# All late output projections moved ahead of the first up-projection, and the token operands of the second pair of chunks made early and kept in DRAM

## The chip, the cores and the metric

The kernel runs on one core of a Trainium2 chip. The metric is the device time of one execution in microseconds (us), as the median of several runs. TensorE is called PE below, VectorE DVE, ScalarE ACT, GpSimd POOL, and SyncE, whose queue issues every DMA of this kernel, SP.

## The reference, cut to what matters

One encoder layer on x of 2048 tokens x 1024 features, float32 throughout:

```python
mix = token_mixer(x, w_in, b_forget, rel_bias, w_out)   # two kinds of attention, 16 heads; y = heads; y @ w_out
x = layer_norm(alpha * x + mix, ln1_g, ln1_b)           # "norm 1"
u = x @ w_up                                            # (1024, 5632)
u = sum(shift(u, j) * conv_w[j] for j in range(3)) + conv_b   # causal, along the tokens
value, gate = split(u, 2)
ffn = (value * gelu(gate)) @ w_down                     # (2816, 1024)
x = layer_norm(alpha * x + ffn, ln2_g, ln2_b)
```

## The kernel before, in words

**Products.** Every float32 operand of a large product is split in two parts of a reduced float32 format (`split`: ACT copies the high part, L177; DVE or POOL subtracts it from the source for the low part, L180), and `mm3` (L184 to L186) makes three matmuls of 128x128 by 128x512 for each product of tiles. A tile is 128 x 512 float32, 256 KB. Which of DVE and POOL makes a low part or a sum is decided while the program is written out, by `choice`, which keeps an estimated load for both.

**Tokens.** The 2048 tokens are four chunks of 512 (0 to 3). Attention comes first, woven with the input projection and then with the output projections of chunks 0 and 1 (`dense_work`, L1221). What remains of this dense work when the attention has been written out, some 41 yields of eight to an output step, is run by the loop `while dense.step()` near the end of the file.

**Output projection.** `out_steps(c)` gives eight steps (2 halves of the columns by 4 blocks of 128 tokens), each of 24 matmuls. Its first step's `load` fetches eight tile pairs of `w_out` (from the DRAM copy `wo_d`, L769) and eight tiles of the attention's output (`y_d`, L777); its `prepare` splits the eight y tiles; its `multiply` does the matmuls and adds the residual. The last step calls `done`, which queues `out_norm(c)` as chores: four for the norm itself (L832, L815, L817, L818, store to `x1_d`), and eight with four PE transposes each (L841), whose results are stored to `x1t_d` in DRAM, tokens along the free axis.

**Up-projection.** `ffn_up2(ca)` multiplies two chunks at once in seven products instead of eight (a Strassen form). It needs seven sets of four token operands: `tokens_step(n)`, for n = 1, 5, 6, 3, 7, 2, 4, loads four tiles of `x1t_d` (L916) for four of the n, makes differences for four of the n (`subtract`, L904), and splits four tiles. These 28 pairs of parts stay in fast memory through the whole up-projection: 22 blocks of seven product steps, each step 12 matmuls. A block loads four tiles of `w_up` (L1012), makes sums of them (L987) and splits, convolves (L855 to L857) and stores h to `h_d`. `ffn_down2(ca)` follows with 77 steps of 12 matmuls, with weights from `wd_d` (L1134) and h from `h_d` (L1131); its norm is `finish` (L1100 to L1115), run as chores.

**Order.** `Pipeline` runs a list of steps. Before step i it calls `load` of steps up to i+5 (beyond i+2 only if enough slots are free) and `prepare` up to i+2; after step i it pops one chore (more in the first seven steps, `PACE`). The list before is: out steps of chunk 2, up-projection of chunks 0 and 1, out steps of chunk 3, down-projection of chunks 0 and 1, up-projection of chunks 2 and 3, down-projection of chunks 2 and 3. The token steps stand in it at positions `FPOS` around the first step of the first up-projection and at `XPOS` (-6, -4, -2, 0, 1, 2, 3) around that of the second. `OLEAD` is the length of the leading part.

**Slots.** All these tiles live in 85 numbered slots (`Slots`): 54 that exist from the start, and 31 on the right side that are added when the attention's buffers go, at the end of the attention, with a key 40 counts later. `get` takes the free slot with the oldest key (`mem.next = 0`). A new user of a slot waits for the last reader of the one before.

**An early start that is written in.** While the remaining dense work runs, `if n == FIRST` (60) would load and split for the first step of the pipeline, from the far end of the list of free slots.

Of the kernel before, what the change touches and what calls it, by code (L numbers as in the profile page):

```python
# [19 lines left out]
P = 128  # L20
# [5 lines left out]
CH = 512  # L26
# [70 lines left out]
OLEAD = 8  # L97
RIGHT_T, FIRST = 40, 60
# [8 lines left out]
def hymba_layer(  # L107
# [61 lines left out]
    wd_d = tl(dram, [NF // 2, 8, 2, P, CH], F32, "wd_d")  # L169

# [589 lines left out]
    def out_steps(c, mem, zp, banks, state, done):  # L760
# [9 lines left out]

        def product_step(j, t):
            def load():
                if (j, t) == (0, 0):
                    load_tiles(0, range(KT))
                    for k in range(KT):
                        ys.append(mem.get())
                        nc.sync.dma_start(ys[k], y_d[k, :, cs])  # L777
                if (j, t) == (0, TQ - 1):
                    load_tiles(1, range(WNEXT))

            def prepare():
                if (j, t) == (0, 0):
                    state["z"] = [{} for _ in range(TQ)]
                    state["stt"] = tl(zp, [P, TQ, 2, 6], F32, "bn", 2)
                    for k, raw in enumerate(ys):
                        ys[k] = mem.get(F32R), mem.get(F32R)
                        split(*ys[k], raw, nc.scalar, nc.vector)
                        mem.put(raw)
# [31 lines left out]
    def out_norm(c, mem, zp, banks, sink, gains, state):  # L820
# [8 lines left out]
        for t in range(TQ):  # L829
            for j in range(2):  # L830
# [4 lines left out]
                nc.sync.dma_start(x1_d[r0 : r0 + P, CH * j : CH * j + CH], zj)  # L835
            yield YT
# [59 lines left out]
    def ffn_up2(ca, fs, mem, banks, before, wide):  # L896

        HK = KT // 2  # L900
        xs = {}
# [4 lines left out]
        b, t2 = {}, {}  # L906

        def tokens_step(n):


            def load():
                for i, q in {1: ((0, 0),), 5: ((0, 1),), 6: ((1, 1),), 2: ((1, 0),)}.get(n, ()):
                    for k in range(HK):
                        before(ca + q, HK * i + k)
                        b[i, q, k] = mem.get()
                        nc.sync.dma_start(f32(b[i, q, k]), x1t_d[ca + q, HK * i + k])  # L916

            def source(k):

                b00, b01, b10, b11 = (b.get((i, q, k)) for i in range(2) for q in range(2))  # L920
                if n == 1:
                    return b00, ()
                if n == 5:
                    t2[k] = b00
                    subtract(b00, b01, b00)
                    return b00, ()
                if n == 6:
                    subtract(t2[k], b11, t2[k])
                    return t2[k], ()
                if n == 3:  # L930
                    return b11, ()
                if n == 7:
                    subtract(b01, b11, b01)
                    return b01, (b01, b11)
                if n == 2:
                    return b10, ()
                subtract(t2[k], b10, t2[k])
                return t2[k], (t2[k], b10)

            def prepare():  # L940
                for k in range(HK):
                    src, last = source(k)
                    xs[n, k] = mem.get(F32R), mem.get(F32R)
                    split(*xs[n, k], f32(src), nc.scalar, choice.engine())
                    mem.put(*last)
# [229 lines left out]
    with ExitStack() as st:  # L1175
# [16 lines left out]
        written = set()  # L1192
# [18 lines left out]
        def normed(c, state):  # L1211
            def done():
                later(out_norm(c, mem, zp, banks, to_dram(c), gains, state), KT + TQ + 1)
                if c == NCH - 1:
                    chores.append(load_norms)
            return done
# [50 lines left out]
        for c in range(2, NCH):  # L1267
            state = {}
            outs.append(out_steps(c, mem, zp, banks, state, normed(c, state)))
        outs = outs[0] + outs[1]  # L1270
# [85 lines left out]
```

## Time and profile before

| | us |
|---|---|
| median of three runs | 2845.57 (2844.66 to 2853.41) |
| profiled execution | 2845.75 |
| its span, first to last instruction | 2843.8 |
| PE busy in the span | 2740.9 (96%) |
| DVE busy | 1933.6 (68%) |
| ACT busy | 1175.7 (41%) |
| POOL busy | 897.4 (32%) |

The 1.95 us between the profiled execution's time and its span lie outside the first and last instruction. PE is busy almost everywhere, but a matmul's recorded time overlaps that of the next one, so what a stretch loses is better read from how many matmuls it holds than from its busy share. Times in the rows are counted from the start of the span. The weight load of PE (PEld) is a row of its own in the views. The granted clock (PEclk) is 1.00 where PE has its full 2.4 GHz.

### The profile page before, as it was taken

To read this page: it belongs to the slowest core of one execution; us is meant where nothing else is said; L and a number is where in the kernel's file an instruction comes from. 1 tells how busy PE (TensorE), PEld (TensorE's weight loads), DVE (VectorE), ACT (ScalarE), POOL (GpSimd) and SP (SyncE) were. 2 spreads that over 40 slices of the span, in tenths; PEclk is the share of its full clock that TensorE was granted. 3 is DMA by queue.
4 is the path that set the end of the run, shared out by engine and by line. 5 is a ranking of instruction groups with operands and counts; after the bars stand their busy time and mean duration, and the time that the engine had idled before them with its cause. 6 is when DMAs were issued, how large, how long until landed. Compare 5 with 4: busy or idle time off the path is not lost.

```text
span 2843.8 us, 38496 instructions
## 1 busy us (share of the span) xinstructions
PE 2740.9 (96%) x12632; PEld 2046.2 (72%) x12632; DVE 1933.6 (68%) x3391; ACT 1175.7 (41%) x2036; POOL 897.4 (32%) x940
## 2 busy tenths in 40 slices
PE   8899999999999999999879999999998999999998
PEld 7675757675666766765657888888876778888886
DVE  4456576767676755567587777765569877777548
ACT  4434344444444443424245544542223545544222
POOL 2224242426557554334152112111026311110012
PEclk9999999999999999999999999999999999999999
DMA  7665667765456445767842222279873322226964
GB/s 236 197 208 179 204 189 222 217 190 184 149 167 195 151 130 152 214 187 232 296 156 78 81 87 78 78 247 327 296 229 114 104 78 84 83 78 206 316 221 163
DMA packets 308487, 498.01 MB, mean 175 GB/s; under 512 B 68896, under 2 KB 84384, under 8 KB 308288
## 3 DMA queue, kind: packets, MB, share of 16 engines
q1 hardware_dynamic: 308288, 495.56, 55.3%
q8 instruction: 100, 1.64, 0.2%
q14 instruction: 99, 0.81, 0.1%
HBM read 347.97 MB, written 147.46 MB: 174 GB/s over the span
## 4 chain that ended last, share of the span: by engine, by line
PE 64%; DVE 6%; issue 3%; DMA 3%; POOL 2%; ACT 1%; SPq 0%; POOLq 0%; DVEq 0%; ACTq 0%
PE acc L184 17%; PE acc L186 17%; PE acc L185 17%; PE y L705 5%; PE sc L581 3%; PE st L618 3%; PE st L619 2%; DVE slot L180 2%; DMA qb<-qh_d 1%; DVE slot L1109 1%; PE sc L657 1%; DMA slot<-y_d 1%; DVE slot L815 1%; ACT slot L177 0%; PE acc L841 0%
## 5 line engine op out<-in xcount | busy, mean ns | idle before, releaser
L184 PE MATMUL acc<-slot,slot 128*128 128x512 f32 (+2 forms) x3128 | 1189.6, 380 | 46.3 <-ACT slot L177 30.2
L186 PE MATMUL acc<-slot,slot 128*128 128x512 f32 (+2 forms) x3128 | 1184.5, 379 | 12.2 <-DVE slot L180 10.6
L185 PE MATMUL acc<-slot,slot 128*128 128x512 f32 (+2 forms) x3128 | 1182.3, 378 | 0.0
L184 PEld LDWEIGHTS acc<-slot,slot 128*128 128x128 f32 x3128 | 594.2, 190 | 171.6 <-ACT slot L177 35.8
L177 ACT ACTIVATE slot<-slot 128x512 fp32r<-128x512 f32 (+1 forms) x688 | 410.3, 622 | 730.0 <-DVE slot L1079 143.2
L186 PEld LDWEIGHTS acc<-slot,slot 128*128 128x128 f32 x3128 | 592.8, 190 | 138.5 <-DVE slot L180 20.0
L185 PEld LDWEIGHTS acc<-slot,slot 128*128 128x128 f32 x3128 | 594.0, 190 | 113.4 <-issue 3.2
L180 DVE TENSOR_TENSOR slot<-slot,slot 128x512 fp32r<-128x512 f32 (+1 forms) x548 | 448.2, 828 | 255.4 <-ACT slot L177 227.1
L639 POOL TENSOR_TENSOR sums<-sums,pt 128x512 f32<-128x512 f32 (+3 forms) x416 | 421.2, 1012 | 237.8 <-ACT pt L630 182.7
L630 ACT ACTIVATE pt<-st 128x512 f32<-128x512 f32 (+3 forms) x544 | 262.2, 492 | 329.6 <-PE st L619 119.2
L180 POOL TENSOR_TENSOR slot<-slot,slot 128x512 fp32r<-128x512 f32 (+1 forms) x144 | 197.6, 1374 | 304.1 <-ACT slot L177 249.0
L705 PE MATMUL y<-pt,vv 128*64 128x512 f32 (+3 forms) x1088 | 280.3, 505 | 0.2 <-DVE yt L647 0.2
L618 PE MATMUL st<-qa,ka 128*128 128x512 f32 (+2 forms) x544 | 208.5, 386 | 8.3 <-ACT pt L630 8.3
L581 PE MATMUL sc<-kb,qb 66*128 66x512 f32 (+2 forms) x544 | 186.8, 373 | 11.8 <-DMA qb<-qh_d 5.2
L619 PE MATMUL st<-qb,kb 97*128 97x512 f32 (+2 forms) x544 | 189.9, 357 | 3.7 <-ACT qb L599 3.3
L584 DVE TENSOR_REDUCE mx<-sc 128x1 f32<-128x512 f32 x192 | 127.8, 685 | 74.5 <-PE sc L581 73.3
L618 PEld LDWEIGHTS st<-qa,ka 128*128 128x128 f32 x544 | 102.5, 189 | 96.8 <-issue 43.7
L705 PEld LDWEIGHTS y<-pt,vv 128*64 128x64 f32 x1088 | 81.6, 136 | 120.4 <-issue 105.1
L856 DVE SCALAR_TENSOR_TENSOR v<-u,cw,v 128x1024 f32<-128x1024 f32 x88 | 113.5, 1290 | 76.4 <-ACT v L855 76.3
L581 PEld LDWEIGHTS sc<-kb,qb 66*128 66x128 f32 x544 | 98.9, 190 | 83.5 <-DVE mx L589 19.8
L639 POOL TENSOR_TENSOR sums<-pt 128x384 f32<-128x384 f32 (+1 forms) x64 | 78.7, 1229 | 251.4 <-PE sc L657 194.8
L589 DVE CUSTOM_DVE_ANT_0 junk<-sc,bq 128x512 bf16<-128x512 f32 (+2 forms) x224 | 108.3, 483 | 47.8 <-PE sc L581 39.0
(113 smaller groups left out, 2263.9 us busy)
## 6 DMA issues: line engine op xcount, KB each, us to landing
slot<-wd_d SPq DMA_DIRECT2D x308, 256.0 KB
slot<-in_w_up_dram SPq DMA_DIRECT2D x176, 256.0 KB
wd_d<-w_hl SPq DMA_DIRECT2D x77, 512.0 KB
slot<-wo_d SPq DMA_DIRECT2D x128, 256.0 KB
h_d<-v SPq DMA_DIRECT2D x44, 512.0 KB
slot<-h_d SPq DMA_DIRECT2D x88, 256.0 KB
slot<-in_w_qk_dram SPq DMA_DIRECT2D x66, 256.0 KB
kb<-kh_d SPq DMA_DIRECT2D x88, 128.0 KB
```

What stands on the lines that cost most here:

```text
L177: nc.scalar.activation(hi, src, AF.Copy)
L180: lo_eng.tensor_tensor(lo, src, f32(hi), op=ALU.subtract)
L184: nc.tensor.matmul(acc, wh, mh, start=first, stop=False, **more)
L185: nc.tensor.matmul(acc, wh, ml, start=False, stop=False, **more)
L186: nc.tensor.matmul(acc, wl, mh, start=False, stop=last, **more)
L581: nc.tensor.matmul(sc[:, m0:m1], qb[:KR, tq], kb[:KR, m0:m1], start=True, stop=True)
L584: nc.vector.tensor_reduce(m, sc[:, k0:k1], axis=AX.X, op=ALU.max)
L618: nc.tensor.matmul(st[:, w2], ka[:, js], qa[:, w2], start=True, stop=False)
L619: nc.tensor.matmul(st[:, w2], kb[:KM, js], qb[:KM, w2], start=False, stop=True)
L630: nc.scalar.activation(pt[:, w], st[:, w], AF.Exp)
L639: nc.gpsimd.tensor_tensor(acc[:, w], (acc if first is None else first)[:, w], pt[:, w], op=ALU.add)
L705: nc.tensor.matmul(y[half, w], v, pt[:, w], start=first and n < 2, stop=last and n >= len(tiles) - 2)
```

## The change

All sixteen output steps of chunks 2 and 3 now stand ahead of the first up-projection, in one list. `out_norm` yields twice more between its norm and its transposes (`NORM_LAG`), and that of chunk 3 is popped at every second step. After it, chores at every third step (`XEVERY`) run a new generator, `store_tokens(2)`: it loads the 16 tiles of chunks 2 and 3 from `x1t_d`, makes the seven sets of operands, splits them, and stores the 56 parts to a new DRAM tensor `xq_d`. The token steps of the second up-projection only load these 56 parts. Making the operands has become a function, `token_operands`, which both users share. `FIRST` is 12 instead of 60, and what happens there is only the loading and splitting of chunk 2's y tiles (`load_y`, `split_y`), from the near end of the list of free slots; the `wo_d` tiles are loaded by the pipeline's own first step.

The part left out of the diff is the old body of `source`, which stands again, with n as an argument, in `token_operands`.

```diff
--- before.py
+++ after.py
@@ -94,8 +94,9 @@
 EV1, EV0 = 2, 3
 PACE = 5, 5, 3, 2, 2, 2, 2
 FPOS = -1, 0, 1, 2, 3, 4, 5
-OLEAD = 8
-RIGHT_T, FIRST = 40, 60
+XEVERY = 3
+RIGHT_T, FIRST = 40, 12
+NORM_LAG = 2
 XPOS = -6, -4, -2, 0, 1, 2, 3


@@ -167,6 +168,8 @@

     wo_d = tl(dram, [KT, 2, 2, P, CH], F32, "wo_d")
     wd_d = tl(dram, [NF // 2, 8, 2, P, CH], F32, "wd_d")
+
+    xq_d = tl(dram, [8, KT // 2, 2, P, CH], F32, "xq_d")

     halo = tl(consts, [P, 2, NF, 2], F32, "halo")
     cw = tl(consts, [P, 2, NF, 4], F32, "cw")
@@ -768,24 +771,33 @@
                 for n in range(2):
                     nc.sync.dma_start(f32(ws[j, k][n]), wo_d[k, j, n])

+        def load_y():
+            for k in range(KT):
+                ys.append(mem.get())
+                nc.sync.dma_start(ys[k], y_d[k, :, cs])
+
+        def split_y():
+            state["z"] = [{} for _ in range(TQ)]
+            state["stt"] = tl(zp, [P, TQ, 2, 6], F32, "bn", 2)
+            for k, raw in enumerate(ys):
+                ys[k] = mem.get(F32R), mem.get(F32R)
+                split(*ys[k], raw, nc.scalar, nc.vector)
+                mem.put(raw)
+
+        state["early"] = load_y, split_y
+
         def product_step(j, t):
             def load():
                 if (j, t) == (0, 0):
                     load_tiles(0, range(KT))
-                    for k in range(KT):
-                        ys.append(mem.get())
-                        nc.sync.dma_start(ys[k], y_d[k, :, cs])
+                    if not ys:
+                        load_y()
                 if (j, t) == (0, TQ - 1):
                     load_tiles(1, range(WNEXT))

             def prepare():
-                if (j, t) == (0, 0):
-                    state["z"] = [{} for _ in range(TQ)]
-                    state["stt"] = tl(zp, [P, TQ, 2, 6], F32, "bn", 2)
-                    for k, raw in enumerate(ys):
-                        ys[k] = mem.get(F32R), mem.get(F32R)
-                        split(*ys[k], raw, nc.scalar, nc.vector)
-                        mem.put(raw)
+                if (j, t) == (0, 0) and "z" not in state:
+                    split_y()

             def multiply():
                 acc = banks.get()
@@ -834,6 +846,8 @@
                 r0 = c * CH + t * P
                 nc.sync.dma_start(x1_d[r0 : r0 + P, CH * j : CH * j + CH], zj)
             yield YT
+        for _ in range(NORM_LAG):
+            yield YT
         for k in range(KT):
             tps = banks.get()
             for t in range(TQ):
@@ -893,56 +907,101 @@
     def nothing():
         pass

-    def ffn_up2(ca, fs, mem, banks, before, wide):
-
-
-
-        HK = KT // 2
-        xs = {}
+    HK = KT // 2
+
+    def token_operands(ca, ks, mem, before, dst):
+
+
+        b, t2 = {}, {}

         def subtract(o, x, y):
             choice.engine().tensor_tensor(f32(o), f32(x), f32(y), op=ALU.subtract)

-        b, t2 = {}, {}
+        def load(i, q):
+            for k in ks:
+                before(ca + q, HK * i + k)
+                b[i, q, k] = mem.get()
+                nc.sync.dma_start(f32(b[i, q, k]), x1t_d[ca + q, HK * i + k])
+
+        def source(n, k):
+
+            b00, b01, b10, b11 = (b.get((i, q, k)) for i in range(2) for q in range(2))
+            if n == 1:
+                return b00, ()
+            if n == 5:
+                t2[k] = b00
+                subtract(b00, b01, b00)
+                return b00, ()
+            if n == 6:
+                subtract(t2[k], b11, t2[k])
+                return t2[k], ()
+            if n == 3:
+                return b11, ()
+            if n == 7:
+                subtract(b01, b11, b01)
+                return b01, (b01, b11)
+            if n == 2:
+                return b10, ()
+            subtract(t2[k], b10, t2[k])
+            return t2[k], (t2[k], b10)
+
+        def load_for(n):
+            for i, q in {1: ((0, 0),), 5: ((0, 1),), 6: ((1, 1),), 2: ((1, 0),)}.get(n, ()):
+                load(i, q)
+
+        def prepare(n):
+            for k in ks:
+                src, last = source(n, k)
+                parts = mem.get(F32R), mem.get(F32R)
+                split(*parts, f32(src), nc.scalar, choice.engine())
+                mem.put(*last)
+                dst(n, k, parts)
+
+        return load_for, prepare
+
+    def store_tokens(ca, mem, before, stored):
+
+
+        def dst(n, k, parts):
+            for l in range(2):
+                nc.sync.dma_start(xq_d[n, k, l], f32(parts[l]))
+            mem.put(*parts, delay=DLY_E)
+            stored.add((n, k))
+
+        for k in range(HK):
+            load, prepare = token_operands(ca, [k], mem, before, dst)
+            for n in UP_ORDER:
+                load(n)
+            for n in UP_ORDER:
+                yield
+                prepare(n)
+
+    def ffn_up2(ca, fs, mem, banks, before, wide, stored):
+
+
+
+        xs = {}
+
+        def keep(n, k, parts):
+            xs[n, k] = parts
+
+        load_tokens, prepare_tokens = token_operands(ca, range(HK), mem, before, keep)

         def tokens_step(n):


             def load():
-                for i, q in {1: ((0, 0),), 5: ((0, 1),), 6: ((1, 1),), 2: ((1, 0),)}.get(n, ()):
-                    for k in range(HK):
-                        before(ca + q, HK * i + k)
-                        b[i, q, k] = mem.get()
-                        nc.sync.dma_start(f32(b[i, q, k]), x1t_d[ca + q, HK * i + k])
-
...
             def prepare():
-                for k in range(HK):
-                    src, last = source(k)
-                    xs[n, k] = mem.get(F32R), mem.get(F32R)
-                    split(*xs[n, k], f32(src), nc.scalar, choice.engine())
-                    mem.put(*last)
+                if not stored:
+                    prepare_tokens(n)

             return Step(load, prepare, nothing, 12 if n in (1, 5, 6, 2) else 8, 0)

@@ -1189,7 +1248,7 @@
                 written.add((c, k))
             return sink

-        written = set()
+        written, stored = set(), set()

         def before(c, k):

@@ -1210,9 +1269,10 @@

         def normed(c, state):
             def done():
-                later(out_norm(c, mem, zp, banks, to_dram(c), gains, state), KT + TQ + 1)
+                later(out_norm(c, mem, zp, banks, to_dram(c), gains, state), KT + TQ + NORM_LAG + 1, 2 if c == NCH - 1 else 1)
                 if c == NCH - 1:
                     chores.append(load_norms)
+                    later(store_tokens(2, mem, before, stored), HK * (len(UP_ORDER) + 1), XEVERY)
             return done

         def dense_work():
@@ -1265,26 +1325,24 @@

         outs = []
         for c in range(2, NCH):
-            state = {}
-            outs.append(out_steps(c, mem, zp, banks, state, normed(c, state)))
-        outs = outs[0] + outs[1]
-        first, up01 = ffn_up2(0, range(NF), mem, banks, before, wide)
-        second, up23 = ffn_up2(2, range(NF), mem, banks, before, wide)
-        lead = place(outs[:OLEAD] + up01, first, [OLEAD + i for i in FPOS])
+            part = {}
+            outs += out_steps(c, mem, zp, banks, part, normed(c, part))
+            if c == 2:
+                early = part["early"]
+        first, up01 = ffn_up2(0, range(NF), mem, banks, before, wide, False)
+        second, up23 = ffn_up2(2, range(NF), mem, banks, before, wide, True)
+        lead = place(outs + up01, first, [len(outs) + i for i in FPOS])
         down01 = ffn_down2(0, mem, zp, banks, gains, later, False)
         down23 = ffn_down2(2, mem, zp, banks, gains, later, True)
         rest = place(down01 + up23, second, [len(down01) + i for i in XPOS])
-        work = Pipeline(mem, lead + outs[OLEAD:] + rest + down23, chores)
+        work = Pipeline(mem, lead + rest + down23, chores)
         mem.add(st.enter_context(tc.tile_pool(name="r_s", bufs=1, **side)), SLOTS_B, RIGHT_T)
         n = 0
         while dense.step():
             n += 1
             if n == FIRST:
-                mem.next = -1
-                work.ahead(-AHEAD_L)
-                work.steps[0].prepare()
-                work.prepared = 1
-                mem.next = 0
+                for fn in early:
+                    fn()
         banks.add(st.enter_context(tc.tile_pool(name="r_ps", bufs=8 - DACC, space=PSUM, **side)), 8 - DACC)
         work.run()
```

## Rows read from the trace of the kernel before

**Rows 1.** The page, part 1: busy us, share and instructions of two engines.
```profile
PE 2740.9 (96%) x12632; PEld 2046.2 (72%) x12632; DVE 1933.6 (68%) x3391; ACT 1175.7 (41%) x2036; POOL 897.4 (32%) x940
```

**Rows 2.** Windows of 50 us: length, PE, PEld, DVE, ACT, POOL busy (count), PEclk, DMA.
```profile
1700.00:1750.00 50.00, 50.00 (x217) 40.51 (x216) 38.29 (x45) 25.75 (x37) 7.64 (x14) 1.00 0.26 79
1900.00:1950.00 50.00, 50.00 (x218) 40.64 (x217) 33.22 (x47) 11.96 (x19) 6.20 (x5) 1.00 0.91 324
...
2100.00:2150.00 50.00, 44.40 (x188) 34.95 (x186) 50.00 (x70) 13.83 (x24) 21.86 (x13) 0.97 0.72 233
...
2600.00:2650.00 50.00, 50.00 (x217) 40.49 (x216) 31.53 (x41) 19.18 (x28) 1.29 (x1) 1.00 0.97 346
```

**Rows 3.** Windows cut at the ends of the losing stretches, and a steady one, same columns.
```profile
1381.00:1397.00 16.00, 8.99 (x28) 5.53 (x29) 15.04 (x19) 7.13 (x13) 6.62 (x4) 0.89 0.94 338
...
1439.20:1497.90 58.70, 40.70 (x165) 30.70 (x164) 47.55 (x55) 30.00 (x54) 37.82 (x25) 0.88 0.38 126
...
1550.00:1850.00 300.00, 300.00 (x1295) 242.78 (x1295) 228.38 (x263) 148.81 (x216) 57.88 (x92) 1.00 0.26 81
...
2093.70:2298.60 204.90, 183.03 (x745) 142.33 (x744) 184.58 (x224) 87.24 (x139) 86.49 (x60) 0.96 0.42 131
```

**Rows 4.** Timeline of PE at chunk 2's first matmul, with the idle time before it.
```profile
1385.53 0.80 PE L184 MATMUL acc<-slot,slot 128*128 128x512 f32 x1 [4.83 <-ACT slot L177]
...
1396.61 0.66 PE L841 MATMUL acc<-ident,slot 128*128 128x128 f32 x4
```

**Rows 5.** Timeline of SP's queue from 1359 to 1384 us: start, us, DMA issues.
```profile
1359.03 0.38 SPq L666 DMA_DIRECT2D y_d<-yt  x1
...
1362.01 7.68 SPq L769 DMA_DIRECT2D slot<-wo_d  x10
...
1375.97 2.69 SPq L769 DMA_DIRECT2D slot<-wo_d  x6
1378.71 5.43 SPq L777 DMA_DIRECT2D slot<-y_d  x8
```

**Rows 6.** Timeline of DVE at chunk 2's y splits.
```profile
1387.51 7.45 DVE L180 TENSOR_TENSOR slot<-slot,slot 128x512 fp32r<-128x512 f32 x5
```

**Rows 7.** What PE waited for, 1439 to 1498 us: total, times, longest.
```profile
PE acc L841 <- POOL slot L818: 4.7, 2, 4.3
...
PE acc L841 <- DVE slot L815: 3.0, 2, 2.5
```

**Rows 8.** DVE's, then POOL's groups, 2095 to 2270 us: count, busy us, mean ns.
```profile
L180 DVE TENSOR_TENSOR slot<-slot,slot 128x512 fp32r<-128x512 f32 x61 | 55.5, 932 | 5.7 <-ACT slot L177 5.5
...
L904 DVE TENSOR_TENSOR slot<-slot,slot 128x512 f32<-128x512 f32 x8 | 7.4, 951 | 0.0
...
L180 POOL TENSOR_TENSOR slot<-slot,slot 128x512 fp32r<-128x512 f32 x20 | 32.2, 1617 | 28.1 <-ACT slot L177 28.1
...
L904 POOL TENSOR_TENSOR slot<-slot,slot 128x512 f32<-128x512 f32 x8 | 12.6, 1584 | 7.2 <-DMA slot<-wd_d 4.1 <-DMA slot<-x1t_d 1.8 <-DVE slot L180 1.2
```

**Rows 9.** Timelines of DVE and POOL in the steady up-projection.
```profile
1707.48 0.69 DVE L180 TENSOR_TENSOR slot<-slot,slot 128x512 fp32r<-128x512 f32 x1
...
1712.01 1.58 DVE L180 TENSOR_TENSOR slot<-slot,slot 128x512 fp32r<-128x512 f32 x1
...
1711.54 1.51 POOL L180 TENSOR_TENSOR slot<-slot,slot 128x512 fp32r<-128x512 f32 x1 [1.94 <-ACT slot L177]
```

**Rows 10.** DVE's group of low parts, 1550 to 1850 us.
```profile
L180 DVE TENSOR_TENSOR slot<-slot,slot 128x512 fp32r<-128x512 f32 x77 | 67.6, 877 | 39.2 <-ACT slot L177 37.5
```

**Rows 11.** Timelines of SP and PE: one block's weights, and that block's first matmul.
```profile
1713.07 8.23 SPq L1012 DMA_DIRECT2D slot<-in_w_up_dram  x4
...
1737.27 0.39 PE L184 MATMUL acc<-slot,slot 128*128 128x512 f32 x1
```

**Rows 12.** Timeline of SP: first and last token loads for the second up-projection.
```profile
2113.19 1.27 SPq L916 DMA_DIRECT2D slot<-x1t_d  x1
...
2164.91 3.97 SPq L916 DMA_DIRECT2D slot<-x1t_d  x4
```

More of the change, by code (lines that the diff above doesn't have):

```diff
@@ L908, in tokens_step @@
         def tokens_step(n):
             def load():
-                for i, q in {1: ((0, 0),), 5: ((0, 1),), 6: ((1, 1),), 2: ((1, 0),)}.get(n, ()):
-                    for k in range(HK):
-                        before(ca + q, HK * i + k)
-                        b[i, q, k] = mem.get()
-                        nc.sync.dma_start(f32(b[i, q, k]), x1t_d[ca + q, HK * i + k])
[L918 to L938, printed above, removed]
@@ L940, in prepare @@
-            def prepare():
-                for k in range(HK):
-                    src, last = source(k)
-                    xs[n, k] = mem.get(F32R), mem.get(F32R)
-                    split(*xs[n, k], f32(src), nc.scalar, choice.engine())
-                    mem.put(*last)
+                if not stored:
+                    load_tokens(n)
+                    return
+                for k in range(HK):
+                    xs[n, k] = mem.get(F32R), mem.get(F32R)
+                    for l in range(2):
+                        nc.sync.dma_start(f32(xs[n, k][l]), xq_d[n, k, l])
@@ L947, in tokens_step @@
+            def prepare():
+                if not stored:
+                    prepare_tokens(n)
             return Step(load, prepare, nothing, 12 if n in (1, 5, 6, 2) else 8, 0)
```

## Prediction

> **What bounds the kernel now.** I read the page first. PE is busy in 2740.9 us of the 2843.8 us span, 96% [rows 1]; the change adds or removes no matmul, so it can only act on what PE loses between matmuls. Windows show where that is. A steady stretch of the first up-projection holds 1295 matmuls in 300 us, 0.2317 us each [rows 3]; in windows of 50 us that is 217 or 218, as at 1700 and at 1900 [rows 2]. The reader is to see that the second of these, where chunk 3's output projection stands between the first up- and down-projection, loses nothing there.
>
> Three stretches lose. (a) Chunk 2's first output step: 28 records in 16 us [rows 3], 24 matmuls (5.6 us) and four transposes (0.4 us, from their start to the next matmul at 1397.03) [rows 4]; 10 us lost. (b) The start of the first up-projection: 58.7 us hold 165 records [rows 3], eleven steps of 12 matmuls, 132 x 0.2317 = 30.6 us, and 33 transposes at 0.1 us, 3.4 us; 24.7 us lost. (c) The end of the first down-projection and the start of the second up-projection: 745 matmuls, 172.6 us of work, in 204.9 us [rows 3]; 32.3 us lost. Together 67 us. The granted clock is 0.89, 0.88 and 0.96 in them [rows 3]: it falls because PE waits, and what that costs is in these sums.
>
> Then the waits. In (a) PE sat 4.83 us for ACT's copies of y [rows 4], and y was fetched only from 1378.71 on [rows 5]. With some 41 yields of dense work left, the test n == 60 never holds: the early start written into the kernel does not happen. In (b) 7.7 us are transposes that wait for chunk 2's norm [rows 7]; the rest is waiting for operands. In (c) DVE is busy 50.00 of 50 us from 2100 [rows 2]: there DVE is the bound, not PE.
>
> **Part 1: y of chunk 2 at yield 12.** Twelve yields of eight to a 5.4 us step after the attention's last matmul is about 1361 us; the last y is stored at 1359 [rows 5]. Slots: ten `wo_d` loads went out at once from 1362 and six waited until 1376 [rows 5], so about ten old slots are free, plus four not yet taken by residuals. The early y takes them, and y is split by some 1376, in a stretch where POOL leaves DVE alone; before, five of these low parts took 7.45 us [rows 6] beside chunk 1's norm. But the ten early `wo_d` loads lose their slots and now wait for chunk 1's last step, as the six did: all sixteen start at 1376. The steady rate seen is 346 GB/s [rows 2], 0.76 us a tile, and one step needs a pair every 0.7 us: sixteen tiles take 12 us, so the last pair comes near 1390 and the step ends near 1391 instead of 1396.6. I take a gain of 5 us; bounds 0 (the tiles are as late as y was) and 10 (all of it).
>
> **Part 2: chunk 3's steps follow chunk 2's.** Their first step needs 24 tiles and is loaded two steps ahead, 10.9 us, against 24 x 0.76 = 18 us of transfer. SP runs ahead of PE where slots are free, so part of it goes earlier; but chunk 2's own 16 second-half tiles and chunk 1's stores are in the same queue. I take a loss of 3 us; bounds 0 and 10. Taking the steps away from their old place saves nothing, as that place lost nothing [rows 2]; the down-projection's first loads have the quiet end of the up-projection as cover (DMA 0.26 busy [rows 2]).
>
> **Part 3: the start of the first up-projection.** Chunk 2's norm is now popped beside chunk 3's output steps, one chore per 5.4 us step with two idle pops before the transposes: the 7.7 us of waiting transposes [rows 7] go. Chunk 3's norm begins after chunk 2's fifteen chores, at the fourth product step, and then at every second step. What stays is making 28 parts and 16 differences on DVE and POOL against PE's 2.8 us a step, with chunk 3's norm falling into its second half. I take a gain of 7 us; bounds 0 (the norm is only moved inside the stretch) and 15 (half of what then remains goes too).
>
> **Part 4: `store_tokens` beside the up-projection.** 28 splits and 16 differences over 96 steps, 267 us. At 0.69 us alone [rows 9] that is 30 us on DVE, which is idle for 72 us in 300 [rows 3], 64 in 267; ACT is half idle (25.75 us busy in 50 [rows 2]). DMA: 16 loads and 56 stores, 18.9 MB in 267 us, 71 GB/s on top of 81 [rows 3] where 346 was seen [rows 2]. In SP's order a store can hold back a block's weights behind it, but those are issued 24.2 us before use (1713.07 to 1737.27, the fifteenth block by count) [rows 11]. Slots: counting the code, 12 to 18 of the 85 are free in this loop; four raw tiles and two parts leave at least 6, and at 3.4 new slots a step six fewer make the weights 5 us later, which 24 us covers. I take a loss of 4 us, since queues are bunched; bounds 0 and 15.
>
> One mechanism speaks against this part. A low part on DVE takes 0.69 us alone and 1.58 us when a POOL one runs, ending 0.54 us after POOL's [rows 9]: it waited; the mean of 77 is 877 ns [rows 10]. If the two engines serialize throughout, their 286 us in 300 [rows 3], less 14 us of such waiting (77 x 0.187), leave 28 us in 300, 25 in 267; the added 44 operations need 30 us on DVE, 66 if all ran at POOL's 1.5 [rows 9]. The excess is 5 to 41 us. I use its lower end in the 4 above, because `choice` sent 77 of this stretch's low parts to DVE [rows 10], of some 108 (seven in each of 15.4 blocks), and keep the mechanism as a rival.
>
> The Trainium skill, "SBUF — State Buffer", section "Who interferes with whom", states this as a rule: a DVE instruction with two inputs in SBUF contends with a GpSimd instruction that reads SBUF, and the second to issue is blocked until the first ends. The two timelines agree with it. By the rule alone the sum would have 5 to 41 us here in place of 4.
>
> **Part 5: the second up-projection's operands are loaded.** In (c) 28 of the 81 low parts (DVE 61, POOL 20) [rows 8] are the tokens'. On DVE that is 21 x 0.932 = 19.7 us and the eight differences' 7.4 us: 27 us; on POOL 7 x 1.617 + 12.6 = 24 us [rows 8]. DVE's 184.6 us become 157.6, below the 172.6 us that PE needs [rows 3]: DVE is no longer the bound, only bunched by `finish`. I keep 7 of the 32.3 us.
>
> What is late next is DMA: 56 tiles, 14.7 MB, instead of 16. Token loads began at 2113 and ended at 2165 [rows 12]; without the stalls the first product starts some 12 us sooner than before, near 2158. From 2113 to 2158 other traffic takes about 170 GB/s of the 233 [rows 2] (12 token tiles among them), leaving 176 of 346: 7.9 MB, 30 tiles. The other 26 need 23 us at about 292 GB/s, and the last set is used in the eighth step, 19.5 us in: 4 us late. So 11 us are kept and 21 gained; bounds 8 (15 of DMA waits and 9 of DVE) and 32.
>
> **Sum**, against the profiled execution's 2845.75 us (2843.8 and 1.95 around it; the median of the runs is 0.18 lower): -5 + 3 - 7 + 4 - 21 = -26, 2819.75; with the median, 2820 us.
>
> **Rivals.**
> 1. The token reads come late: slots are freed only step by step, so most of (c) stays. For: 56 tiles want slots while 22 of h are held; against: the old loads ran some 16 us ahead of PE. Gain 8 in place of 21: 2833.
> 2. DVE and POOL serialize in the up-projection [rows 9, 10]; midway, 20 us in place of 4: 2836. Against: the excess is zero if few of the added operations go to POOL.
> 3. Chunk 3's 24 loads wait behind chunk 2's, and PE sits through the 18 us: 2835 if none is hidden. Against: SP issues long before PE comes.
> 4. Slower than before: the slots taken by `store_tokens`, and before it by chunk 3's z held until about the thirtieth step, make each block's weights late. It decides once the lead of 24.2 us [rows 11] falls below the 5 us or so of landing, sum and split; then each block loses, and 1.2 us a block over 22 blocks cancels the gain. At 1.7 us a block it is 37 us: 2857. Against: the count leaves 15 us of lead or more.
> 5. The change does not do what it says: DVE's peaks only move, from (c) into (b) and the loop, and the gains cancel: 2845.
>
> **How the numbers follow.** Forecast 0.54; rivals 1: 0.15, 2: 0.12, 3: 0.07, 4: 0.08, 5: 0.04. The forecast's own range is 2808 to 2832. Two in ten lie outside 2802 to 2843: rivals 4 and 5 above, and below that the upper bounds of parts 1, 3 and 5 together. A measurement tells about 0.3%, 8.5 us, from no change. Faster: the forecast and nearly all of rivals 1 to 3, some of which fall within 8.5 us when two meet: 0.80; same 0.11 (those, and rival 5); slower 0.09.
>
> **What would show it.** Y loads of chunk 2 in SP's queue near 1361, and a shorter idle time before its first matmul, now ended by a `wo_d` tile. No transposes waiting for POOL near 1490. Blocks at 19.5 us between 1550 and 1850, with DVE near 43 us in 50. In the stretch that answers to (c), DVE below 92% busy, no L904, 56 loads of `xq_d`, and PE waits, if any, ended by DMA. Wrong it would be if blocks of the first up-projection grow longer, or if PE waits over 15 us for `xq_d`.

## The result, and the profile after

| | before | after |
|---|---|---|
| median, runs of one session | 2850.72 us | 2829.05 us (2822.33 to 2835.15, 5 runs) |
| ratio | | 0.9928, 95% interval 0.9905 to 0.9951 |
| profiled execution, its span | 2845.75, 2843.8 us | 2829.05, 2827.3 us |

The change makes the kernel 0.7% faster. The page's first part after it, to be read beside [rows 1]: PE's busy time is the same within 1.4 us, and its share rises; DVE lost 11 us and POOL 37.

```profile
PE 2739.5 (97%) x12632; PEld 2046.1 (72%) x12632; DVE 1922.9 (68%) x3415; ACT 1174.1 (42%) x2033; POOL 860.7 (30%) x916
```

Windows of the changed kernel, with the columns of [rows 3]. They are cut where a stage's first product begins: the last ten dense groups of twelve matmuls, chunk 2's output steps, chunk 3's, the first 60 us of the first up-projection, 98 of its later steps, and the stretch around the start of the second one.

```profile
1352.70:1385.10 32.40, 30.17 (x132) 24.53 (x131) 19.99 (x32) 8.34 (x13) 0.21 (x4) 0.95 0.87 298
1385.10:1432.80 47.70, 47.70 (x226) 39.39 (x225) 19.26 (x29) 8.07 (x15) 6.43 (x4) 1.00 0.96 347
1432.80:1479.60 46.80, 46.80 (x214) 38.01 (x212) 36.37 (x57) 15.11 (x26) 8.47 (x6) 1.00 0.88 311
1479.60:1540.00 60.40, 44.84 (x167) 33.13 (x165) 58.98 (x59) 32.44 (x54) 37.67 (x27) 0.86 0.41 135
1626.00:1905.00 279.00, 274.50 (x1178) 220.09 (x1178) 225.25 (x275) 149.66 (x224) 66.31 (x87) 1.00 0.41 138
2082.30:2290.80 208.50, 199.34 (x830) 157.07 (x829) 160.12 (x218) 77.39 (x118) 44.50 (x38) 0.98 0.57 193
```

Chunk 2's steps now fill their window: PE is busy in all of its 47.70 us at clock 1.00, where before the 16 us around their first step held 28 records [rows 3]. The start of the up-projection is as bad as it was: 167 records in 60.40 us against 165 in 58.70, and DVE is busy in 58.98 of the 60.40, where it was in 47.55 of the 58.70 [rows 3]. What PE waited for most from 1478 to 1545 us are low parts made by DVE (total, times, longest):

```profile
PE acc L189 <- DVE slot L183: 8.7, 4, 4.9
```

All kernels here run the same 504 groups of twelve matmuls after the attention, so a stage can be followed from kernel to kernel by counting groups back from the last matmul. The lengths below are worked out in that way from each kernel's own profiled execution; the first column is when the attention ends. It differs by up to 6 us between kernels that are the same up to there (1347.8 in e3, 1354.0 in e6), so the stages tell more than the whole times do. The rest, marked with dots, is the last 14 steps of the first up-projection, the last 112 of the second and the second down-projection: 574.1 to 575.7 us in every kernel.

```
              attn.  dense  out   out   up01  up01   down01  down01   up23   rest  span
              end    10 gr  c2    c3    1-42  43-140 1-50    51-77    1-42
before        1353.1  32.4  53.6  44.4  145.0  272.7  142.3    87.6  136.8  ...   2843.8
after         1352.7  32.3  47.7  46.8  146.5  278.9  138.4    80.9  127.6  ...   2827.3
e1 no early   1353.9  34.8  53.3  46.3  146.9  278.0  138.6    81.1  126.9  ...   2834.8
e2 own tokens 1349.8  32.2  47.7  46.8  146.8  272.0  138.5    87.6  136.0  ...   2832.7
e3 norm late  1347.8  30.1  47.7  46.8  143.0  279.9  138.5    81.2  126.9  ...   2817.0
e4 xpos early 1348.6  32.4  47.7  46.8  146.5  278.5  138.4    91.0  124.3  ...   2829.1
e5 dve start  1353.1  29.8  47.8  46.8  140.5  278.3  138.4    80.9  127.6  ...   2818.2
e6 w first    1354.0  29.7  47.7  46.8  147.0  278.8  138.4    79.6  125.1  ...   2822.6
e7 82 slots   1352.4  30.3  47.7  46.8  147.8  279.3  138.5    78.0  131.7  ...   2826.5
e8 before+    1351.6  27.6  63.2  44.7  140.4  271.8  143.8    87.5  136.7  ...   2842.6
e9 lag 0      1356.6  28.0  49.9  47.7  143.8  278.0  138.6    80.4  127.7  ...   2826.2
e10 stagger   1348.0  30.6  47.9  47.0  146.9  274.8  138.7    81.3  126.9  ...   2817.6
e11 combo     1353.3  29.9  47.7  46.8  140.3  275.0  138.7    81.1  124.3  ...   2812.5
e12 combo 2   1353.2  29.8  47.7  46.8  141.2  275.1  138.7    79.8  125.3  ...   2813.0
```

The span's 16.5 us are: dense and chunk 2 -6.0, chunk 3 +2.4, up-projection start +1.4, its loop +6.2, down-projection -3.9, the stretch at the second up-projection -6.7 and -9.2, and -0.7 elsewhere. Most of +2.4, +1.4 and -3.9 is norm transposes, at 0.1 us each, that moved with chunk 3: 32 left the down-projection, 20 now stand in chunk 3's steps, the up-projection's first 42 steps hold 44 instead of 32, and 8 of chunk 0's, moved by `NORM_LAG`, now stand in the dense groups. The dense groups ran at a granted clock of 0.95 in this profiled execution and took 32.3 us, 2.2 of them a wait of the transposes; in e10, the same up to there and with the same wait, the clock was 1.00 and they took 30.6. Among the kernels that are the same up to there, dense groups and chunk 2 together take 77.4 to 78.5 us in e3, e5 to e7 and e10 to e12, and 79.9 to 80.1 in e2, e4 and the changed kernel. So up to 2.6 us more are won there in other executions than this trace shows.

### The profile page after: what moved, and what is told of

It is laid out like the page before. It is cut to its first block, busy times and chain, and to the rows that moved or that the text cites. A ratio compares the mean times of both kernels' runs of the same rounds, so it can differ in the third digit from the quotient of the medians.

```text
span 2827.3 us, 38720 instructions
## 1 busy us (share of the span) xinstructions
PE 2739.5 (97%) x12632; PEld 2046.1 (72%) x12632; DVE 1922.9 (68%) x3415; ACT 1174.1 (42%) x2033; POOL 860.7 (30%) x916
## 5 line engine op out<-in xcount | busy, mean ns | idle before, releaser
L183 DVE TENSOR_TENSOR slot<-slot,slot 128x512 fp32r<-128x512 f32 (+1 forms) x570 | 432.1, 769 | 251.5 <-ACT slot L180 222.8
L183 POOL TENSOR_TENSOR slot<-slot,slot 128x512 fp32r<-128x512 f32 (+1 forms) x122 | 168.0, 1378 | 274.5 <-ACT slot L180 193.2
```

The lines of the kernel that those rows point to most:

```text
L183: lo_eng.tensor_tensor(lo, src, f32(hi), op=ALU.subtract)
```

## The experiments

Each kernel's ratio is to the kernel before, timed in the same session. E1 to e4 ran in one session, e5 to e8 and e9 to e12 in two others, without the changed kernel beside them; so what an edit is worth against the changed kernel is read from the stages.

**E1: no early y.**
```diff
-RIGHT_T, FIRST = 40, 12
+RIGHT_T, FIRST = 40, 1000
```


> The changed kernel with the early loading and splitting of chunk 2's y switched off (its yield number is never reached). Theory, the early y carries what was won ahead of chunk 2: PE waits 4 us or more for y at chunk 2's first matmul, its first step takes some 10 us in place of 5.5, and the time is 6 us above the changed kernel's (1 to 10). Rival, what was won there comes from the transposes moved by NORM_LAG and the other order: the time stays within 2 us of the changed kernel's.

Measured: 2838.59 us, ratio 0.9965 (0.9950 to 0.9980). The dense groups and chunk 2's steps take 88.1 us against 80.0, and chunk 2's first output step 11.2 against 5.5. The timeline of PE at chunk 2's first matmuls in e1 has the row of [rows 4] back:

```profile
1388.65 0.66 PE L187 MATMUL acc<-slot,slot 128*128 128x512 f32 x1 [4.34 <-ACT slot L180]
```

The theory held, at the upper end of its 1 to 10 us: 8.1 by the stages, some 10 by the ratios. The changed kernel's queue of SP shows the early loads, and that the `wo_d` tiles were not late either: they went out from 1372.80 on, 12 us before their use.

```profile
1364.25 4.91 SPq L777 DMA_DIRECT2D slot<-y_d  x8
...
1372.80 15.50 SPq L772 DMA_DIRECT2D slot<-wo_d  x22
```

**E2: the second up-projection makes its own operands.**
```diff
-        second, up23 = ffn_up2(2, range(NF), mem, banks, before, wide, True)
+        second, up23 = ffn_up2(2, range(NF), mem, banks, before, wide, False)
-                    later(store_tokens(2, mem, before, stored), ...)
```


> The changed kernel, but the second up-projection loads and splits its own token operands as before, and nothing is stored beside the first. Theory: the stretch from the last 27 steps of the down-projection to the 42nd step of the second up-projection takes 16 us longer again (208.5 to about 224 us), the 98 steps of the first up-projection from its 43rd on take 6 us less (278.9 to about 273), in sum 10 us above the changed kernel. Rival, the stretch became shorter because chunk 3's output projection and norm no longer stand ahead of the down-projection: the stretch stays near 208 us and the time falls by 6 us.

Measured: 2838.29 us, ratio 0.9961 (0.9948 to 0.9974). The stretch is 223.6 us against 208.5, the loop 272.0 against 278.9: the theory in both. The window that answers to [rows 2], first in e2, then in the changed kernel:

```profile
2100.00:2150.00 50.00, 43.27 (x175) 34.24 (x174) 49.94 (x62) 20.11 (x34) 26.55 (x16) 0.90 0.67 222
```
```profile
2100.00:2150.00 50.00, 49.83 (x216) 40.53 (x217) 49.32 (x79) 13.42 (x21) 8.03 (x5) 1.00 0.79 264
```
DVE is full in both. In the changed kernel it gets 79 operations done instead of 62, and PE loses nothing: 216 records against 175. So a DVE that is busy all the time is not yet what PE waits for; it depends on what stands in its queue. DVE's low parts and norm in e2, from 2080 to 2260 us (count, busy us, mean ns):

```profile
L183 DVE TENSOR_TENSOR slot<-slot,slot 128x512 fp32r<-128x512 f32 x61 | 53.5, 899 | 5.6 <-ACT slot L180 5.4
L1168 DVE SCALAR_TENSOR_TENSOR slot<-slot,mv,slot 128x512 f32<-128x512 f32 x16 | 23.5, 1498 | 0.0
```
The same two groups in the changed kernel, from 2085 to 2260 us, where POOL has 22 operations on whole tiles instead of 49:
```profile
L183 DVE TENSOR_TENSOR slot<-slot,slot 128x512 fp32r<-128x512 f32 x47 | 35.5, 767 | 15.5 <-ACT slot L180 14.4 <-PE acc L188 0.9
...
L1168 DVE SCALAR_TENSOR_TENSOR slot<-slot,mv,slot 128x512 f32<-128x512 f32 x16 | 13.4, 865 | 0.0
```
Sixteen norm operations that the change does not touch fall from 1498 to 865 ns: taking the tokens away freed DVE of more than their own time.

**E3: chunk 3's norm 18 steps later.**
```diff
             def done():
+                if c == NCH - 1:
+                    chores.extend([nothing] * 18)
```


> The changed kernel with 18 idle chores ahead of chunk 3's norm, so that it begins some 18 product steps later. Theory, the start of the first up-projection is bound by DVE and POOL, and chunk 3's norm (17 us of DVE, 7 of POOL) falls into it: its first 42 steps take 10 to 15 us less than 146.5, and so does the whole. Rival, it is bound by slots: the eight z tiles of chunk 3 are held 18 steps longer, the first blocks' weights are issued less than 10 us before use, and the 42 steps take 146 us or more.

Measured: 2828.41 us, ratio 0.9916 (0.9898 to 0.9934); the first 42 steps take 143.0 us, 3.5 less: neither theory's number. DVE's timeline in e3 says why the edit did little:

```profile
1465.43 1.81 DVE L844 SCALAR_TENSOR_TENSOR slot<-slot,mv,slot 128x512 f32<-128x512 f32 x1
...
1504.79 3.38 DVE L844 SCALAR_TENSOR_TENSOR slot<-slot,mv,slot 128x512 f32<-128x512 f32 x2
```
Chunk 3's norm (L844) begins in DVE's queue at 1465.43, before the first product step (1472.5), and goes on at 1504.79 beside the sixth (1501.3 to 1506.0); popped 18 steps later, it should have begun behind the eighteenth. Against the changed kernel its first two operations did not move at all, and the other six by some 14 us. A chore's place in the list is not its place in an engine's queue; that the framework that places the instructions moved them forward is a reading, which no run isolates.

In the same stretch of e3 a sum on POOL took 5.80 us, while DVE ran back to back, and PE waited longest for a low part on POOL (total, times, longest):

```profile
1481.19 5.80 POOL L1046 TENSOR_TENSOR slot<-slot,slot 128x512 f32<-128x512 f32 x1 [3.69 <-DVE slot L183]
```
```profile
PE acc L189 <- POOL slot L183: 7.2, 2, 4.6
```

**E4: token loads of the second up-projection six places earlier.**
```diff
-XPOS = -6, -4, -2, 0, 1, 2, 3
+XPOS = -12, -10, -8, -6, -4, -2, 0
```


> The changed kernel with the token loads of the second up-projection placed at -12, -10, -8, -6, -4, -2, 0 instead of -6, -4, -2, 0, 1, 2, 3. Theory, what is still lost there (some 16 us) is token tiles issued too late, 24 of the 56 after the first product could start: the stretch of 208.5 us becomes 5 to 10 us shorter, with no PE wait for tokens. Rival, the earlier tiles take slots and transfer time from the down-projection's weights: PE waits there instead, and the stretch takes 208 us or more.

Measured: 2833.61 us, ratio 0.9950 (0.9932 to 0.9969). The rival held: the up-projection's start gains 3.3 us and the end of the down-projection loses 10.1, waiting for its own weights. Whether these are late behind the tokens in SP's queue or for want of the slots that the tokens hold was not told apart. What PE waited for there, in e4:

```profile
PE acc L187 <- DMA slot<-wd_d: 8.8, 4, 3.3
```

**E5: DVE alone at the start of the first up-projection.**
```diff
+    def on(dve):
+        return choice.fixed(nc.vector) if dve else choice.engine()
 # token_operands: differences and low parts
-    choice.engine()
+    on(ca == 0)
 # block_steps: weight sums and low parts
-    choice.engine()
+    on(ca == 0 and f < 3)
```


> The changed kernel with all low parts and differences of the first up-projection's token operands, and the weight sums and low parts of its first three blocks, on DVE; POOL has only its share of the norms there. Theory, a POOL operation of 1.3 to 1.8 us keeps a DVE operation with two inputs in fast memory waiting (and waits itself), so 20 of them cost more than the 0.68 us each that DVE needs alone: the first 42 steps (146.5 us) take 8 to 15 us less. Rival, the two engines work side by side and DVE is simply full there: it gets some 14 us more work, and the 42 steps take 150 to 160 us.

Measured: 2820.04 us, ratio 0.9890 (0.9871 to 0.9910). The first 42 steps take 140.5 us, 6.0 less, where the seven kernels that keep this stretch as it is take 146.5 to 147.8: the theory's direction, at three quarters of its least size. DVE's low parts and differences from 1460 to 1545 us, first in the changed kernel, then in e5:

```profile
L183 DVE TENSOR_TENSOR slot<-slot,slot 128x512 fp32r<-128x512 f32 x30 | 24.8, 860 | 1.0 <-ACT slot L180 1.0
L918 DVE TENSOR_TENSOR slot<-slot,slot 128x512 f32<-128x512 f32 x13 | 14.4, 1137 | 0.0
```
```profile
L183 DVE TENSOR_TENSOR slot<-slot,slot 128x512 fp32r<-128x512 f32 x44 | 28.7, 681 | 3.8 <-ACT slot L180 3.6
L921 DVE TENSOR_TENSOR slot<-slot,slot 128x512 f32<-128x512 f32 x16 | 10.3, 680 | 0.0
```
DVE does 60 operations in 39.0 us where 43 took 39.2: the help of POOL was worth nothing to DVE there. The Trainium skill, "SBUF — State Buffer", section "Who interferes with whom", has it as a rule that a DVE instruction with two inputs in SBUF contends with a GpSimd instruction that reads SBUF. The trace agrees: 680 ns each with hardly any POOL work beside it, 860 and 1137 with it.

**E6: the first block's weights ahead of the tokens.**
```diff
+        tokens, weights0 = second[0].load, up23[0].load
+        def both():
+            weights0()
+            tokens()
+        second[0].load, up23[0].load = both, nothing
```


> The changed kernel with the four weight tiles of the second up-projection's first block loaded ahead of its first token tiles, not behind most of them. Theory, what PE still loses there comes first from these four tiles, which are issued behind 32 token loads (ACT waits 14.9 us for them, and its queue behind it): the stretch of 208.5 us becomes 4 to 7 us shorter. Rival, it is the token tiles or the down-projection's norm that come last: the stretch stays within 2 us.

Measured: 2827.21 us, ratio 0.9916 (0.9898 to 0.9935); the stretch is 204.7 us, 3.8 shorter, just under the theory's 4. Timeline of SP and of ACT in the changed kernel, where the four weight tiles come behind 32 token loads, the last eight of them shown, and ACT's queue stands for them:

```profile
2151.66 5.04 SPq L1000 DMA_DIRECT2D slot<-xq_d  x8
2157.01 2.41 SPq L1071 DMA_DIRECT2D slot<-in_w_up_dram  x4
2159.72 16.66 SPq L1000 DMA_DIRECT2D slot<-xq_d  x24
```
```profile
2162.52 0.63 ACT L180 ACTIVATE slot<-slot 128x512 fp32r<-128x512 f32 x1 [14.93 <-DMA slot<-in_w_up_dram]
```
**E7: three slots fewer.**
```diff
-SLOTS_A, SLOTS_B = 54, 31
+SLOTS_A, SLOTS_B = 54, 28
```


> The changed kernel with 82 slots instead of 85. Theory, the 6 us that the first up-projection loses beside the storing of tokens (98 steps, 278.9 us against 272.7) come from slots: weights are issued only 13 us before use, ACT waits for them, and PE for ACT's copies behind; three slots fewer make that 288 us or more, while the second up-projection's 112 steps, with nothing beside them, stay at 312 us. Rival, they come from DVE and POOL holding each other up: it stays at 279 us.

Measured: 2835.21 us, ratio 0.9943 (0.9923 to 0.9963); the 98 steps take 279.3 us against 278.9, the second up-projection's 311.3. In blocks 7 to 18, where the storing goes on, the last of a block's four weight tiles is issued 8.3 to 10.8 us before the block's first product, instead of 10.7 to 14.3, and the time stays. Slots do not make the loop's loss. That leaves DVE and POOL, the rival; it does not yet say how.

**E8: the kernel before with its early start reached.**
```diff
-RIGHT_T, FIRST = 40, 60
+RIGHT_T, FIRST = 40, 12
-                work.ahead(-AHEAD_L)
+                work.steps[0].load()
+                work.loaded = 1
```


> The kernel before, with its early start reached: at the twelfth remaining yield the first step's w_out and y tiles are loaded, and y split, from the far end of the free slots. Theory: that alone takes away the loss ahead of chunk 2 (the ten dense groups and chunk 2's sixteen take 86 us in before, 80 in the changed kernel), 6 to 10 us faster than before. Rival, the slots at the far end are free only after the attention, and other loads are delayed by these: less than 2 us.

Measured: 2847.31 us, ratio 0.9989 (0.9975 to 1.0003): nothing. The dense groups lose their wait (27.6 us), but chunk 2's steps take 63.2. Its y went out behind sixteen `wo_d` tiles, at 1371.23 against 1364.25 in the changed kernel, and the low parts end at 1389 against 1377, so chunk 1's norm comes behind them, and meets POOL. DVE's and POOL's timeline in e8, and what PE waited for:

```profile
1371.23 5.06 SPq L777 DMA_DIRECT2D slot<-y_d  x8
```
```profile
1392.19 6.58 DVE L815 SCALAR_TENSOR_TENSOR slot<-slot,sd,slot 128x512 f32<-128x512 f32 x4
```
```profile
1391.92 6.29 POOL L818 TENSOR_TENSOR slot<-slot,slot 128x512 f32<-128x512 f32 x4 [30.14 <-ACT slot L817]
```
```profile
PE acc L841 <- DVE slot L815: 6.5, 4, 4.2
```
The wait for y became a wait of the transposes for the norm. The 4.8 us that the two stages lose (90.8 against 86.0) come back at the first up-projection's start, 140.4 us against 145.0; why was not looked into.

**E9: no idle pops.**
```diff
-NORM_LAG = 2
+NORM_LAG = 0
```


> The changed kernel with NORM_LAG 0: the transposes of a norm follow it at once. Theory, an early y alone only moves the wait (the kernel before with an early start has its transposes waiting for chunk 1's norm inside chunk 2's steps); the two idle pops are what lets PE use it: the dense rest and chunk 2 (80.0 us together) take 84 to 90 us. Rival, the idle pops do nothing here: 80 us.

Measured: 2825.02 us, ratio 0.9903 (0.9886 to 0.9920). The two stages take 77.9 us, within what other kernels with the early y take (77.4 to 80.1): the theory fell. The idle pops are not what makes the early y useful. What is left of the difference to e8 is that y goes out ahead of the `wo_d` tiles, and into other slots; which of the two weighs more was not told apart.

**E10: the store chores at gaps of four and three.**
```diff
-                    later(store_tokens(2, ...), HK * (len(UP_ORDER) + 1), XEVERY)
+                    work = store_tokens(2, ...)
+                    for n in range(HK * (len(UP_ORDER) + 1)):
+                        later(work, 1, 4 - n % 2)
```


> The changed kernel with the store chores at gaps of 4 and 3 steps in turn instead of 3, so that each falls at the same two places of a seven-step block, away from one and four steps' distance at which the seven waits of the loop were seen. Theory, the loop's 6 us are DVE's queue: extra operations ahead of a block's convolution delay the gelu and with it ACT's copy of an accumulator for which PE waits; at other places they fit: 98 steps in 273 to 275 us. Rival, the added DVE and POOL time itself is too much wherever it is put: 278 us or more.

Measured: 2823.79 us, ratio 0.9897 (0.9880 to 0.9914). The 98 steps take 274.8 us: 4.1 of the 6.2 us come back, with as many operations in them (50 of the 56 stores go out in these steps, 49 in the changed kernel). But the gaps are also longer on the average, 3.5 steps for 3, and the stores spread over 266 us instead of 235; a run at gaps of 3 with other places, or of 3.5 at the old ones, would tell place from spacing, and there is none. What PE waited for in the loop, in the changed kernel and in e10:

```profile
PE acc L187 <- ACT slot L192: 4.5, 7, 0.8
```
```profile
PE acc L187 <- ACT slot L192: 1.7, 4, 0.5
```
One of the seven, in the timelines of PE and ACT of the changed kernel: PE's next product waits for ACT's copy of an accumulator (L192), which stands behind the gelu, which waited 1.67 us for DVE's convolution.

```profile
1657.70 0.50 PE L187 MATMUL acc<-slot,slot 128*128 128x512 f32 x1 [0.69 <-ACT slot L192]
```
```profile
1656.11 1.06 ACT L1034 ACTIVATE v<-v 128x1024 f32<-128x1024 f32 x1 [1.67 <-DVE v L871]
1657.07 0.58 ACT L192 ACTIVATE slot<-acc 128x512 f32<-128x512 f32 x1
```

**E11: e5, e6 and e10 together.**

> DVE alone for the first up-projection's token operands and first three blocks, the second up-projection's first weights ahead of its tokens, and the store chores at gaps of 4 and 3, all on the changed kernel. If the three act at different places they add: first 42 steps 140.5, the next 98 steps 274, the stretch at the second up-projection 204.5, in sum 14 us below the changed kernel, near 2815. If they disturb each other, 2820 or above.

Measured: 2808.79 us (2805.93 to 2814.31), ratio 0.9849 (0.9830 to 0.9867). The stages add up: -6.2, -3.9 and -3.1 against the changed kernel, 13.2 us, near the 14 expected; the profiled execution, of which these are read, is the longest of the four (2814.31). This is the fastest version, 1.5% below the kernel before.

**E12: DVE alone also at the second start and in chunk 3's norm.**
```diff
-    on(ca == 0 and f < 3)
+    on(f < 3)
 # out_norm
-    scale_add(..., nc.gpsimd if j else nc.vector)
+    scale_add(..., nc.gpsimd if j and c < 3 else nc.vector)
```


> The kernel with the three edits, and DVE alone also for the first three blocks of the second up-projection and for chunk 3's norm. Theory, a POOL operation beside a full DVE costs more than it relieves: the first 42 steps 136 to 139 us, the stretch at the second up-projection 200 to 203 us. Rival, with the tokens off POOL the engines no longer hinder each other, and the added DVE work lengthens both by 2 us or more.

Measured: 2814.34 us, ratio 0.9865 (0.9847 to 0.9883). The 42 steps take 141.2 us against e11's 140.3, the stretch 205.1 against 205.4. Neither number is the theory's, nor the rival's; once the tokens are off POOL, moving the rest gains nothing.

## Why the prediction was right, and where its steps were not

Forecast 2820 us in 2802 to 2843, measured 2829.05, inside its narrower range of 2808 to 2832 as well. The sum of -26 us against the profiled execution came out as -16.7 (2845.75 to 2829.05): parts 3 and 5 were too hopeful, by 7 and 5 us, and part 4 by 2; parts 1 and 2 came out some 4 us better.

- **Part 1** (-5): -6.0 in this trace, and e1 shows it: without the early y the two stages take 88.1 us, 2.1 more than before. The reason given for its size was wrong: the `wo_d` tiles did not wait for chunk 1's last step until 1376, they went out from 1372.80, and PE waited for none of them.
- **Part 2** (+3): no loss. Of the 2.4 us, 2.0 are the 20 transposes that now stand there; chunk 3's 24 tiles were covered.
- **Part 3** (-7): nothing gained, the largest error of the sum. This step failed. The transposes no longer wait, as said, but DVE, busy 58.98 us in 60.40, makes the operands too late, so a wait taken away at one place only let the next operand be the late one. Chunk 3's norm was to fall into the second half of the stretch; its operations on DVE ran from 1472.5 to 1524.7, ahead of the first product and through the first 45 us, and e3 shows that the list's order could not keep it out. E5 shows what the sum left out here: POOL's share of the work made DVE's operations longer, and without it 6.0 us are won. The prediction had this mechanism as a rival for the loop alone. I had the lower bound of this term, 0, as the norm "only moved inside the stretch", and that is what happened.
- **Part 4** (+4): +6.2. The 24.2 us of lead [rows 11] are 27.0, since the matmul at 1737.27 belongs to the last step of the block before; for the last of a block's four tiles it is some 19. Beside the storing that fell to 10.7 to 14.3 us, by 5 to 8 where 5 were counted, and e7 shows that a further fall costs nothing. The loss goes with the place and the spacing of the added operations: e10 gets two thirds of it back. By the prediction's own sign of being wrong, blocks of the first up-projection did grow, from 19.5 to 19.9 us on the average, as its +4 implied. Of the rival by which DVE and POOL serialize, the price came out near its lower end, 5.
- **Part 5** (-21): -15.9. That making the tokens there cost this time is shown by e2. That DVE is the bound because it is busy in 50.00 of 50 us was too simple a reading: it is as full after the change, and PE runs beside it (the second window at e2). What PE waited for most in this stretch before were ACT's copies of accumulators, 11.6 us in seven waits; after the change none of these is left. Of what stays, 3.8 us are neither DVE's bunching nor late token tiles, as the prediction had it, but the first block's four weight tiles behind them in SP's queue (e6). PE waited for no token tile. Loading the tokens earlier only moves the wait to the down-projection's weights (e4).

The prediction says of the granted clock that it falls because PE waits. The dense groups show that this is not all: with the same wait of 2.2 us it was 0.95 in the changed kernel's trace and 1.00 in e10's.

Rival 1, late token reads with a gain of 8 us, did not come true. Rival 4, weights made late by slots, and rival 3, chunk 3's loads, are excluded by e7 and by the window of chunk 3's steps. Rival 5 is true in part: the loop takes back 6.2 us, and the first up-projection's start stayed as long as it was. Two slips in the working, 33 transposes for 32 and 19.7 us for 19.6, change nothing.

## What to carry to other kernels

When two engines share out elementwise work by an estimate of their times, look at the mean of one operation in a stretch that is full: if it grows where both work, the second engine may help nothing, and giving all to the first can be faster (e5: 6 us). Work taken out of a full stretch and put beside another that has room pays, but where and how closely it is set in the cycle of the stage that takes it matters too (e10: 4.1 of 6.2 us), and what is queued behind its loads must be named (e6, e4). An early load has its worth from what it goes out ahead of, what slots it takes and what hangs on it, not from being early as such (e8). An engine's busy share of 100% does not say that another waits for it (e2).

## What the runs showed of the hardware

In e8, four operations on DVE took 6.58 us beside four on POOL that took 6.29, from 1392 to 1399 us. DVE's took 1.55 to 1.75 us each and ended some 0.5 us behind one of POOL's, where the same operation takes DVE 0.74 us in e5 with little beside it; POOL's took 1.27 us for the first and 1.71 for the others. So each waited for the other engine. They took turns for the most part, not wholly: a pair came every 1.7 us, while 0.74 and POOL's 1.27 are 2.0.

The blocking goes both ways. The sum on POOL in e3 that took 5.80 us, from 1481.19 to 1486.99, had DVE beside it, running operations of 0.68 us back to back until 1485.87; it ended 1.1 us after DVE stopped, and the next sum, at 1488.29 with DVE idle, took 1.27 us. That POOL would be the one to starve I had not expected.
